# Queries and keys stored by heads in DRAM, weight transfers issued by SyncE in line with all other transfers

## The chip, the cores and the metric

One core of one Trainium2 chip. The metric is device time in microseconds of one execution of the whole step, median of three runs.

## What is computed

One inference step of a two-layer decoder, for a prompt of 1024 positions and for 8 sample tokens beside it. Each layer projects its input, runs attention on one half of the columns and a recurrent mix (RWKV-7) on the other, and then a feed-forward of width 4096. What the change touches is the path from the projection to attention:

```python
p = x @ w_comb                                   # x: (1024, 1024)
q = p[..., :512].reshape(B, T, 8, 64)
k = p[..., 512:1024].reshape(B, T, 8, 64)
v = p[..., 1024:1536].reshape(B, T, 8, 64)
q, k = rope(q, pos), rope(k, pos)                # halves of 32 of each head are rotated against each other
att = dilated_attention_prompt(q, k, v)          # windows (128,1), (512,4), (2048,16)
...
mix = jnp.concatenate([att, rw], -1) @ lp['w_out']
x1 = layer_norm(DEEPNORM_ALPHA * x + mix, ...)
h = jnp.square(jax.nn.relu(x1 @ lp['w_ff_up'])) @ lp['w_ff_down']
```

## The kernel before, in words

Each layer `l` is worked through in two halves `h` of 512 positions (the second with the 8 sample tokens). All large products are written by `dense_steps` (L365 to L372): the operands are split into a high and a low part of type fp32r, and each 128-row piece takes three matmuls (L370 high x high, L371 high weights x low input, L372 low weights x high input).

**Weights.** `Weights.fill` brings 820 pieces in the order of their use, nearly all 128x512 fp32 (256 KB). Of each, one transfer fills `wr` (L342, three buffers), ACT casts it to the high part `wh` (L343, four buffers), and DVE subtracts to give the low part `wl` (L344, four buffers). The transfer is issued by ACT itself, and `issue_after` puts it behind the cast of the second-last piece in ACT's order. All other transfers are issued by SP (SyncE).

**Order of the work.** TensorE's order is written out by hand: `Streams` merges six streams (dense products, attention, the two stages of the recurrence and others) by a model of their costs. The order on the other engines and on SP is made by the scheduler of the language. Each engine, and SP, works its list in order: what stands at the head and waits holds up what stands behind it.

**Queries and keys.** `in_proj` computes 128 columns of q and k for a pair of heads `p`, as a tile of 128 rows x 512 positions. Because of the rotation the rows lie as (half f, head d, index r), 2 x 2 x 32. L638 stores that tile as it is in `d_qkv[l][h][p, j]` (j = 0 for q, 1 for k), one transfer of 256 KB, 32 in all. `att_load` reads it back by heads: `heads(src)[hd]` picks two blocks of 32 rows of one head, and `stage` (L1497 to L1501) loads those 64 rows twice, once into each half of the 128 partitions of a tile `stg` (two buffers). ACT casts `stg` to the high parts `qS` (L1522) and `kS` (L1526), POOL subtracts to give the low parts (L1523, L1527). In the second half each pair of heads also loads `qf` and `kf` (L1514, L1515), each in two transfers, one a head, and the last 128 keys of the half before. In all there are 160 `stg` transfers (128 of 128 KB, 32 of 32 KB) and 32 of `qf` and `kf`.

```python
def heads(src):
    return src.rearrange("(f d r) t -> d f r t", f=2, d=2)
```

In the names of the rows, `wr`, `wh`, `wl` are a weight piece and its parts; `dps` is a dense product; `d_el`, `BL`, `XB`, `tm`, `X`, `XT` belong to the recurrence's triangular solve, which goes through DRAM several times; `kvc` is the cache of the sample tokens.

Of the kernel before, what the change touches and what calls it, by code (L numbers as in the profile page):

```python
# [28 lines left out]
HB = T // 2  # L29
# [115 lines left out]
class Streams:  # L145
# [24 lines left out]
    def note(self, *key):  # L170
        self.times[key] = self.now

    def after(self, *key, lat=0):
        return lambda: self.times[key] + lat if key in self.times else None
# [73 lines left out]
def body(ctx, tc, I, O):  # L248
    nc = tc.nc
    PE, V, A, G, S = nc.tensor, nc.vector, nc.scalar, nc.gpsimd, nc.sync  # L250
# [22 lines left out]
    def C(name):  # L273
        a, n = CAT[name]
        return cst[:, a:a + n]
# [24 lines left out]
    def both(f):  # L300
        return [[f(l, h) for h in range(2)] for l in range(DEPTH)]
# [5 lines left out]
    d_qkv = both(lambda l, h: dr.tile([4, 3, 128, HB], F32, name=f"d_qkv{l}{h}"))  # L307
# [7 lines left out]
    class Weights:  # L315

        def __init__(self, specs):  # L320
            self.pieces, self.first = [], []
            for srcs, m, dest in specs:
                self.first.append(len(self.pieces))
                self.pieces += [(src, m, dest) for src in srcs]
            self.first.append(len(self.pieces))
            self.out, self.copies = {}, []
            self.nl = self.i = self.kept = 0

        def fill(self, ahead=4):
            at = self.first[self.i]  # L330
            while self.nl < min(len(self.pieces), at + ahead):
                src, m, dest = self.pieces[self.nl]
                if dest is not None:
                    h, lo = dest()
                elif self.kept + sum(p[2] is None for p in self.pieces[at:self.nl]) == 4:
                    break
                else:
                    h = wp.tile([128, 4, 128], F32R, tag="wh", bufs=4, name="wh")
                    lo = wp.tile([128, 4, 128], F32R, tag="wl", bufs=4, name="wl")
                w = wp.tile([128, 4, 128], F32, tag="wr", bufs=3, name="wr")  # L340
                with tc.issue_after(self.copies[-2].ins) if len(self.copies) > 1 else nullcontext():
                    A.dma_start(w[:, :, :m], src)  # L342
                self.copies.append(A.copy(h[:, :, :m], w[:, :, :m]))  # L343
                V.tensor_tensor(lo[:, :, :m], w[:, :, :m], h.bitcast(F32)[:, :, :m], op=ALU.subtract)  # L344
                self.out[self.nl] = (h, lo)
                self.nl += 1
# [32 lines left out]
    def dense(items, kts, xhh, xll, evac):  # L379

        res = []
        yield (0, None, 0, "d")
        yield from dense_steps(items, kts, xhh, xll, res)
        for it, p in zip(items, res):
            r = evac(it, p)
            if r is not None:
                yield r
        for i, it in enumerate(items):
            yield (res[-1] if i == 0 else 0, ("d", 900 + 500 * i), 0, None)
# [8 lines left out]
    def proj_order():  # L398
        seq = [("z", 0)]
        for p in range(4):  # L400
            if p < 3:
                seq.append(("z", p + 1))
            seq.append(("a", p))
        return seq
# [147 lines left out]
    def in_proj(l, h, hook=None, tail=None, then=None):  # L552
# [27 lines left out]
        def z_ev(p, j):  # L580
            def put(c0, n, d):
                S.dma_start(d_z[l][h][p, j, :, c0:c0 + n], d[:, :n])
            return shifted(l, h, muv(4 * j + p), 128, 4 * j + p, put)
# [9 lines left out]
        for cs in ([[c] for c in first] if l > 0 else [ck]):  # L593
            end = cs[-1][0] + cs[-1][1] == HX[h]
            for i in ends[-2:] + ends[:-2] if held else ends:
                m, ev = lo[i]
                keep = not end and i in ends[-2:]
                w = held.pop(0) if held and not keep else W.take(keep)
# [15 lines left out]
        for kind, p in proj_order()[1:]:  # L614
            if kind == "a" and p == 3 and then is not None:
                yield from then()
            for j in range(3):
                w = W.take()
                if kind == "z":
                    ev = z_ev(p, j)  # L620
                    for c0, n in ck:
                        yield from dense([(w, 128, c0, n)], K8, xhc, xlc, ev)
                    continue
                seq = (2 * l + h) * 4 + p
                if j == 1 and seq > 0:
                    yield after("post", seq - 1)
                t = ap_.tile([128, HN[1]], F32, tag="qe", bufs=2, name="qe")

                def eva(it, pt):
                    _, _, c0, n = it  # L630
                    (V.tensor_copy if c0 else A.copy)(t[:, c0:c0 + n], pt[:, :n])
                for c0, n in CK[h]:
                    yield from dense([(w, 128, c0, n)], K8, xhc, xlc, eva)
                if j == 0 and h == 1:
                    t8 = ap_.tile([128, 5, 8], F32, tag="t8", name="t8")
                if j < 2:
                    rope(t, HN[h], tabs)
                    S.dma_start(d_qkv[l][h][p, j], t[:, 0:HB])  # L638
                    if j == 1:
                        S.dma_start(O["k_p"][l, p, :, h * HB:h * HB + HB], t[:, 0:HB])  # L640
                if h == 1 and j == 0:
                    if p == 0:
                        sq[l] = (rq.tile([128, 4, 32], F32, tag="q2", name="q2"), rq.tile([128, 4, 8], F32, tag="kn", name="kn"))
                        G.memset(sq[l][0], 0.0)
                    G.memset(t8[:, 1:4, :], 0.0)
                    for hd in range(2):
                        G.tensor_scalar(sq[l][0][:, p, hd:16:2], t[:, HB:HN[1]], C("hm")[:, hd:hd + 1], None, op0=ALU.mult)
                elif h == 1:
                    G.tensor_scalar(t8[:, (0, 4)[j - 1], :], t[:, HB:HN[1]], 1.0, None, op0=ALU.mult)
                    if j == 1:  # L650
                        G.tensor_scalar(sq[l][1][:, p, :], t[:, HB:HN[1]], 1.0, None, op0=ALU.mult)
            if kind == "a":
                qe[seq] = (l, h, p, t, t8 if h == 1 else None)
                note("qe", seq)
            note(kind, l, h, p)
# [832 lines left out]
    def att_load(l, h, p):  # L1488

        qS, qL, kS = [], [], []

        def heads(src):
            return src.rearrange("(f d r) t -> d f r t", f=2, d=2)

        def stage(src, hd, n):  # L1497
            t = ap_.tile([128, HB], F32, tag="stg", bufs=2, name="stg")[:, :n]
            for x in range(2):
                S.dma_start(t[64 * x:64 * x + 64], heads(src)[hd])  # L1500
            return t  # L1501

        def byres(t):
            return t.rearrange("p (j a c) -> p j c a", a=32, c=4)

        def inrow(t):
            return t.rearrange("p (j c a) -> p j c a", a=32, c=4)

        qf = kf = None
        if h == 1:  # L1510
            qf, kf = (ap_.tile([128, HB], F32, tag=x, name=x) for x in ("qf", "kf"))
            for hd in range(2):
                hs = slice(64 * hd, 64 * hd + 64)
                S.dma_start(qf[hs], heads(d_qkv[l][1][p, 0])[hd])  # L1514
                S.dma_start(kf[hs], heads(d_qkv[l][0][p, 1])[hd])  # L1515
        for hd in range(2):
            hs, ls = slice(64 * hd, 64 * hd + 64), slice(64 - 64 * hd, 128 - 64 * hd)
            q = ap_.tile([128, HB], F32R, tag=f"q{hd}", name="qS")
            ql = ap_.tile([128, HB], F32R, tag=f"ql{hd}", name="qL")
            k = ap_.tile([128, HB + 128], F32R, tag=f"k{hd}", name="kS")  # L1520
            t = stage(d_qkv[l][h][p, 0], hd, HB)
            A.copy(inrow(q), byres(t))  # L1522
            AQ.tensor_tensor(inrow(ql), byres(t), inrow(q.bitcast(F32)), op=ALU.subtract)  # L1523
            for src, c, n in [(d_qkv[l][0][p, 1][:, HB - 128:HB], 0, 128)] * h + [(d_qkv[l][h][p, 1], 128 * h, HB)]:
                t = stage(src, hd, n)
                A.copy(k[:, c:c + n], t)  # L1526
                AQ.tensor_tensor(k[ls, c:c + n], t[ls], k.bitcast(F32)[ls, c:c + n], op=ALU.subtract)  # L1527
            qS.append(q)
            qL.append(ql)
            kS.append(k)  # L1530
        return qS, kS, qL, qf, kf, R.now + 6000 + 1000 * (h + 1)
# [328 lines left out]
```

## Time and profile before

| | us |
|---|---|
| median of 3 runs (lowest, highest) | 3555.35 (3549.26, 3558.99) |
| the profiled execution | 3560.94 |
| its span, first to last instruction | 3559.1 |
| TensorE (PE) busy | 3202.7 (90%) |
| VectorE (DVE) busy | 2055.5 (58%) |
| ScalarE (ACT) busy, issues of transfers not counted | 1448.3 (41%) |
| GpSimd (POOL) busy | 979.3 (28%) |

[...] The profile has one page for the whole run, and views of the trace: who waited for whom, the chain of work that ended last, the instructions in order of time, and busy times of chosen stretches. Queue instructions carry a q (SPq, ACTq): they issue transfers and are not counted as busy. PE is busy in nine tenths of the span, so time is to be had from its idle tenth and from the stretches in which its clock is low.

### The profile page before, as it was taken

Reading aid. Unit: us, or ns where it says so; the run is one execution under the profiler, and the core shown is the slowest. Engines: PE = TensorE matmul, PEld = TensorE weight load, DVE = VectorE, ACT = ScalarE, POOL = GpSimd, SP = SyncE. Lnnn points to the kernel's source line nnn. Section 1 sums busy time; section 2 is a strip of 40 time slices with the busy share of each in tenths; the row PEclk is TensorE's granted clock in tenths of the full one; section 3 lists DMA queues with packets and bytes.
Section 4 is the critical chain, followed back from the end, with each engine's and each line's share of the span. In section 5 each row is a group of like instructions: output and inputs, shape, how many; then the busy total and the mean of one; then the engine's idle time right before and its main releaser. Section 6 shows DMA issues by size and latency. Waiting matters only on the chain. (4 is left out here: it accounts for less than half of the span.)

```text
span 3559.1 us, 65853 instructions
## 1 busy us (share of the span) xinstructions
PE 3202.7 (90%) x24732; PEld 2697.6 (76%) x24732; DVE 2055.5 (58%) x4703; ACT 1448.3 (41%) x3266; POOL 979.3 (28%) x1841
## 2 busy tenths in 40 slices
PE   8788897977999998888999999797797999889998
PEld 6567776765777687677899998685675677789998
DVE  4455554764554664567565457465764564685556
ACT  4345333443343344344443336343443333453334
POOL 2324233531111421435211113334412121340012
PEclk9899998988999999998999999898898999999999
DMA  7334343433443335442333235344243343333332
GB/s 219 107 113 124 115 115 103 129 95 99 117 112 85 106 97 163 139 150 68 86 98 92 80 98 154 117 126 133 71 118 100 111 113 91 117 101 91 94 90 84
DMA packets 366533, 393.55 MB, mean 111 GB/s; under 512 B 141848, under 2 KB 219112, under 8 KB 366216
## 3 DMA queue, kind: packets, MB, share of 16 engines
q10 hardware_dynamic: 121152, 213.44, 20.9%
q1 hardware_dynamic: 245064, 175.92, 16.9%
q8 instruction: 195, 3.19, 0.4%
q14 instruction: 122, 1.00, 0.1%
HBM read 325.30 MB, written 63.97 MB: 109 GB/s over the span
## 5 line engine op out<-in xcount | busy, mean ns | idle before, releaser
L370 PE MATMUL dps<-xh,wh 128*128 128x256 f32 (+3 forms) x2984 | 1006.9, 337 | 31.0 <-ACT xh L758 15.0
L371 PE MATMUL dps<-xl,wh 128*128 128x256 f32 (+3 forms) x2984 | 956.8, 321 | 10.4 <-DVE xl L759 8.6
L372 PE MATMUL dps<-xh,wl 128*128 128x256 f32 (+3 forms) x2984 | 953.3, 319 | 1.2 <-DVE wl L344 1.0
L344 DVE TENSOR_TENSOR wl<-wr,wh 128x512 fp32r<-128x512 f32 (+1 forms) x772 | 581.8, 755 | 501.3 <-ACT wh L343 485.6
L343 ACT CAST wh<-wr 128x512 fp32r<-128x512 f32 (+1 forms) x772 | 475.1, 616 | 844.4 <-PE dps L371 777.8
L370 PEld LDWEIGHTS dps<-xh,wh 128*128 128x128 f32 x2984 | 576.6, 193 | 106.4 <-issue 31.0
L371 PEld LDWEIGHTS dps<-xl,wh 128*128 128x128 f32 x2984 | 576.8, 193 | 46.3 <-DVE xl L759 12.5
L372 PEld LDWEIGHTS dps<-xh,wl 128*128 128x128 f32 x2984 | 575.6, 193 | 41.0 <-DVE wl L344 2.6
L370 PE MATMUL dps<-hh,wh 128*128 128x512 f32 (+2 forms) x1600 | 536.1, 335 | 5.4 <-DVE hh L941 3.6
L371 PE MATMUL dps<-hl,wh 128*128 128x512 f32 (+2 forms) x1600 | 513.1, 321 | 4.5 <-DVE hl L830 3.3
L372 PE MATMUL dps<-hh,wl 128*128 128x512 f32 (+2 forms) x1600 | 512.0, 320 | 0.0
L370 PEld LDWEIGHTS dps<-hh,wh 128*128 128x128 f32 x1600 | 303.5, 190 | 45.2 <-issue 17.7
L371 PEld LDWEIGHTS dps<-hl,wh 128*128 128x128 f32 x1600 | 304.1, 190 | 22.6 <-DVE hl L830 4.1
L372 PEld LDWEIGHTS dps<-hh,wl 128*128 128x128 f32 x1600 | 303.9, 190 | 22.6
L1209 POOL TENSOR_TENSOR tm<-BL,XB 32x15 f32<-32x15 f32 (+7 forms) x480 | 153.0, 319 | 496.5 <-DMA BL<-d_el 375.9
L973 DVE TENSOR_TENSOR t<-dps,t 128x256 f32<-128x256 f32 (+1 forms) x240 | 123.6, 515 | 161.1 <-PE dps L372 160.7
L1211 POOL TENSOR_TENSOR XB<-XB,tm 32x15 f32<-32x15 f32 (+7 forms) x480 | 154.6, 322 | 34.4
L726 POOL TENSOR_TENSOR ln<-ln,lsq 128x256 f32<-128x256 f32 (+1 forms) x112 | 91.2, 814 | 232.5 <-ACT lsq L724 229.9
L941 DVE CAST hh<-rl 128x256 fp32r<-128x256 f32 (+2 forms) x200 | 74.4, 372 | 108.6 <-ACT rl L940 105.4
L939 ACT ACTIVATE rl<-dps 128x256 f32<-128x256 f32 (+2 forms) x200 | 88.4, 442 | 102.2 <-PE dps L372 89.9
L715 POOL TENSOR_TENSOR t<-t,ln 128x256 f32<-128x256 f32 (+1 forms) x32 | 28.1, 913 | 352.1 <-ACT ln L709 352.1
L370 PE MATMUL dps<-hh,xh 128*128 128x256 f32 (+1 forms) x368 | 112.6, 306 | 13.3 <-DVE t L1006 7.2
(345 smaller groups left out, 5098.0 us busy)
## 6 DMA issues: line engine op xcount, KB each, us to landing
wr<-in_w_ff_up ACTq DMA_DIRECT2D x272, 256.0 KB
wr<-in_w_ff_down ACTq DMA_DIRECT2D x256, 256.0 KB
wr<-in_w_in ACTq DMA_DIRECT2D x220, 256.0 KB
stg<-d_qkv SPq DMA_DIRECT2D x128, 128.0 KB
wr<-in_w_out ACTq DMA_DIRECT2D x64, 256.0 KB
z<-d_z SPq DMA_DIRECT2D x24, 384.0 KB
d_qkv<-qe SPq DMA_DIRECT2D x32, 256.0 KB
kvc<-in_cache_k SPq DMA_DIRECT2D x32, 256.0 KB
```

Of the source, the lines that this page charges most:

```text
L343: self.copies.append(A.copy(h[:, :, :m], w[:, :, :m]))
L344: V.tensor_tensor(lo[:, :, :m], w[:, :, :m], h.bitcast(F32)[:, :, :m], op=ALU.subtract)
L370: PE.matmul(p[:m, :n], wh[:, wk % 4, :m], hi, start=(i == 0), stop=False)
L371: PE.matmul(p[:m, :n], wh[:, wk % 4, :m], lo, start=False, stop=False)
L372: PE.matmul(p[:m, :n], wl[:, wk % 4, :m], hi, start=False, stop=(i == last))
L715: G.tensor_tensor(t, t, self.cm[:, c0:c0 + n], op=ALU.subtract)
L726: G.tensor_tensor(s2, s2, sq, op=ALU.add)
L939: A.activation(r, p[:, :n], AF.Relu)
L941: V.tensor_copy(hh[:, c0:c0 + n], r)
L973: V.tensor_tensor(to, p[:, :n], to, op=ALU.add)
L1209: G.tensor_tensor(tv, bc(BL[:, 17 * j + 1:17 * j + 2], [(1, m), (0, j + 1)]), bc(XB[:, 16 * j:16 * j + 1], [(0, m), (1, j + 1)]), op=ALU.mult)
L1211: G.tensor_tensor(xv, xv, tv, op=ALU.add)
```

## The change

The tile of queries or keys is stored in four transfers of 32 rows, so that in DRAM the 64 rows of a head lie together (head d, half f, index r). The reads by head become plain blocks of 64 rows, and `qf` and `kf` become one transfer of 128 rows each. The weight transfers are issued by SP, without the condition on the cast of the second-last piece.

```diff
-            self.out, self.copies = {}, []
+            self.out = {}
...
-                with tc.issue_after(self.copies[-2].ins) if len(self.copies) > 1 else nullcontext():
-                    A.dma_start(w[:, :, :m], src)
-                self.copies.append(A.copy(h[:, :, :m], w[:, :, :m]))
+                S.dma_start(w[:, :, :m], src)
+                A.copy(h[:, :, :m], w[:, :, :m])
                 V.tensor_tensor(lo[:, :, :m], w[:, :, :m], h.bitcast(F32)[:, :, :m], op=ALU.subtract)
...
                     rope(t, HN[h], tabs)
-                    S.dma_start(d_qkv[l][h][p, j], t[:, 0:HB])
+                    for f in range(2):
+                        for d in range(2):
+                            a, b = 64 * f + 32 * d, 64 * d + 32 * f
+                            S.dma_start(d_qkv[l][h][p, j, b:b + 32], t[a:a + 32, 0:HB])
...
-        def heads(src):
-            return src.rearrange("(f d r) t -> d f r t", f=2, d=2)
-
         def stage(src, hd, n):
             t = ap_.tile([128, HB], F32, tag="stg", bufs=2, name="stg")[:, :n]
             for x in range(2):
-                S.dma_start(t[64 * x:64 * x + 64], heads(src)[hd])
+                S.dma_start(t[64 * x:64 * x + 64], src[64 * hd:64 * hd + 64])
...
-            for hd in range(2):
-                hs = slice(64 * hd, 64 * hd + 64)
-                S.dma_start(qf[hs], heads(d_qkv[l][1][p, 0])[hd])
-                S.dma_start(kf[hs], heads(d_qkv[l][0][p, 1])[hd])
+            S.dma_start(qf, d_qkv[l][1][p, 0])
+            S.dma_start(kf, d_qkv[l][0][p, 1])
```

TensorE's order is the same in both kernels. SP's list grows from 1277 to 2177 transfers: 820 weight transfers come to it, the stores of queries and keys go from 32 to 128, `qf` and `kf` from 32 to 16. The three places below show what moves.

SP in the first layer's second half, where the second pair of heads is loaded for attention, before (of the loads of `qf` and `kf` the second pair is shown):

```order
L1514 DMA qf<-d_qkv_109 64x1x512
L1515 DMA kf<-d_qkv_108 64x1x512
L1500 DMA stg<-d_qkv_109 64x1x512 x4
L1399 DMA d_rw_93<-y 128x256
L1500 DMA stg<-d_qkv_108 64x1x128 x2
L1092 DMA lo_8869<-d_lo_105 128x2x264
L1500 DMA stg<-d_qkv_109 64x1x512 x4
```

and now:

```order
L1509 DMA qf<-d_qkv_109 128x512
L1510 DMA kf<-d_qkv_108 128x512
L1497 DMA stg<-d_qkv_109 64x512 x4
L1497 DMA stg<-d_qkv_108 64x128
L1399 DMA d_rw_93<-y 128x256
L1497 DMA stg<-d_qkv_108 64x128
L339 DMA wr<-in_w_ff_up 128x512
L1497 DMA stg<-d_qkv_109 64x512 x2
L339 DMA wr<-in_w_ff_up 128x512
L1092 DMA lo_8911<-d_lo_105 128x2x264
```

The loads keep their places, their shape is now 64x512 in one block, and two weight transfers stand among them, the first behind the store `d_rw<-y`.

SP in the first layer's first half, where a tile of queries is stored, before:

```order
L1215 DMA d_el_115<-XB 32x16x16
L638 DMA d_qkv_108<-qe 128x512
L1220 DMA X<-d_el_115 64x4x64
L1216 DMA d_el_116<-tm 32x16x16
L1220 DMA X<-d_el_115 64x4x64
L1399 DMA d_rw_92<-y 128x256
L1221 DMA XT<-d_el_116 64x4x64 x2
L1500 DMA stg<-d_qkv_108 64x1x512 x2
```

and now:

```order
L1215 DMA d_el_115<-XB 32x16x16
L638 DMA d_qkv_108<-qe 32x512
L1220 DMA X<-d_el_115 64x4x64 x2
L1216 DMA d_el_116<-tm 32x16x16
L638 DMA d_qkv_108<-qe 32x512 x2
L1221 DMA XT<-d_el_116 64x4x64 x2
L638 DMA d_qkv_108<-qe 32x512
L1399 DMA d_rw_92<-y 128x256
L339 DMA wr<-in_w_in 128x512
L1497 DMA stg<-d_qkv_108 64x512 x2
```

The four parts of the store are spread among the transfers of the recurrence, and the last part, `d_rw<-y` and a weight transfer stand ahead of the load.

ACT at the first of these places, before:

```order
L343 CAST wh<-wr 128x512
L1526 CAST kS<-stg 128x512
L342 DMA wr<-in_w_ff_up 128x512
L721 ACTIVATE ln_7566<-t 128x256
L1522 CAST qS<-stg 128x512
L1302 COPY T_7905<-pT_7896 128x256
```

and now:

```order
L1521 CAST kS<-stg 128x512
L724 ACTIVATE lsq<-t 128x256
L1569 ACTIVATE E,mx<-E,mx 128x640
L340 CAST wh<-wr 128x512
L1517 CAST qS<-stg 128x512
L721 ACTIVATE ln_7610<-t 128x256
L1302 COPY T_7947<-pT_7938 128x256
```

The weight transfer that stood behind the cast of the keys is gone from ACT, and the cast of the keys stands three places earlier; the copy `T` that TensorE needs still stands behind the cast of the queries.

## Rows read from the trace of the kernel before

**Rows 1.** The page: busy times, and the chain that ended last by line.

```profile
PE 3202.7 (90%) x24732; PEld 2697.6 (76%) x24732; DVE 2055.5 (58%) x4703; ACT 1448.3 (41%) x3266; POOL 979.3 (28%) x1841
...
PE dps L370 7%; PE dps L371 7%; PE dps L372 7%; DMA stg<-d_qkv 3%; DVE t L756 1%; DMA wr<-in_w_out 0%; PE pS L1554 0%; DVE t L737 0%; DVE wl L344 0%; PE pX L1280 0%; POOL tm L1209 0%; DVE ln L725 0%; PE po L1611 0%; SPq L1500 0%; POOL XB L1211 0%
```

**Rows 2.** The chain that ended last, from 2200 to 2720 us: start, us, what.

```profile
by line: DMA stg<-d_qkv 19.6%; PE dps L370 12.1%; PE dps L372 10.2%; PE dps L371 10.2%; issue 2.8%; PE pS L1554 2.2%; SPq L1500 2.0%; DVE t L737 1.6%; PE pX L1280 1.5%; PE po L1611 1.2%; POOL kS L1527 1.2%; POOL qL L1523 1.2%; PE pS L1565 1
...
2236.54 3.04 DMA d_qkv<-qe
2241.29 12.67 DMA stg<-d_qkv
...
2698.09 7.96 DMA stg<-d_qkv
```

**Rows 3.** Who waited for whom, ACT: total us, times, longest.

```profile
ACT kS L1526 <- DMA stg<-d_qkv: 191.7, 33, 16.6
ACT qS L1522 <- DMA stg<-d_qkv: 120.7, 19, 15.3
```

**Rows 4.** Instructions of ACT, 703 to 731 us: start, us, name, count, idle before.

```profile
709.33 0.60 ACT L343 CAST wh<-wr 128x512 fp32r<-128x512 f32 x1
721.17 0.62 ACT L1526 CAST kS<-stg 128x512 fp32r<-128x512 f32 x1 [11.23 <-DMA stg<-d_qkv]
721.19 0.34 ACTq L342 DMA_DIRECT2D wr<-in_w_ff_up  x1
...
727.53 1.09 ACT L1522 CAST qS<-stg 128x512 fp32r<-128x512 f32 x1 [5.42 <-DMA stg<-d_qkv]
...
728.52 0.37 ACT L1302 COPY T<-pT 128x256 f32<-128x256 f32 x1
```

**Rows 5.** The same stretch on SP's queue.

```profile
704.59 10.31 SPq L1500 DMA_DIRECT2D stg<-d_qkv  x4
```

**Rows 6.** The same stretch on PE.

```profile
728.94 1.12 PE L1280 MATMUL pX<-XT,T 64*64 64x64 f32 x16 [15.38 <-ACT T L1302]
```

**Rows 7.** Busy time in 16 stretches: us, PE, PEld, DVE, ACT, POOL (counts), PEclk, DMA, GB/s.

```profile
263.90:269.40 5.50, 0.00 (x0) 0.00 (x0) 0.00 (x0) 1.29 (x5) 3.24 (x3) 0.96 0.11 37
...
866.10:888.60 22.50, 0.02 (x1) 0.00 (x0) 0.73 (x2) 1.36 (x3) 1.26 (x1) 0.58 0.27 83
...
sum 151.30, PE 0.15 PEld 0.06 DVE 10.05 ACT 28.90 POOL 25.14; mean PE 0.01 PEld 0.00 DVE 0.63 ACT 1.81 POOL 1.57
```

**Rows 8.** The same view of the 16 stretches right behind those.

```profile
328.30:334.30 6.00, 5.08 (x33) 3.69 (x33) 0.84 (x4) 2.90 (x7) 2.37 (x3) 0.50 0.26 68
...
2266.40:2272.40 6.00, 6.00 (x40) 5.96 (x41) 1.52 (x2) 0.46 (x1) 1.74 (x5) 0.77 0.55 170
...
sum 90.40, PE 88.47 PEld 73.37 DVE 41.37 ACT 27.68 POOL 41.12; mean PE 5.53 PEld 4.59 DVE 2.59 ACT 1.73 POOL 2.57
```

**Rows 9.** The chain that ended last: two transfers of the nearest shapes.

```profile
2803.03 2.65 DMA kvc<-in_cache_v
...
2893.37 3.29 DMA ST<-in_state_wkv
```

**Rows 10.** Single lines: count, min/median/max ns of one issue, first and last start.

```profile
L638 SPq DMA_DIRECT2D d_qkv<-qe x32: 319/332/2788, 73.4 to 2430.7; - x32
L1425 SPq DMA_DIRECT2D iup<-in_vres_up x8: 342/576/592, 1123.0 to 2653.3; - x8
L342 ACTq DMA_DIRECT2D wr<-in_w_ff_up x272: 334/334/372, 684.3 to 3500.0; - x136
```

**Rows 11.** Instructions in order of time from 0 us, SP's queue.

```profile
0.72 5.77 SPq L507 DMA_DIRECT2D t<-in_x  x8
```

**Rows 12.** Who waited for whom, POOL: total us, times, longest.

```profile
POOL tm L1209 <- DMA BL<-d_el: 375.9, 24, 50.1
```

**Rows 13.** Who waited for whom, SP's queue: total us, times, longest.

```profile
SPq L1198 <- DVE LB L1191: 179.9, 16, 30.2
SPq L1215 <- POOL XB L1211: 152.4, 28, 17.2
SPq L1399 <- DVE y L1398: 125.1, 25, 12.9
```

## The prediction, made before the changed kernel ran

> **What bounds the kernel now.** I read the page first. PE is busy for 3202.7 us of the 3559.1 us span [rows 1], so the kernel is bound by PE, and what can be won is its 356.4 us of idle time, and the time it works at a low clock. In the chain that ended last one transfer stands out among lines of matmuls: `stg<-d_qkv`, the read of queries and keys, with 3% of the span [rows 1]. The second view is that chain between 2200 and 2720 us, the second layer's attention loads: there `stg<-d_qkv` is the largest item of all, 19.6% of 520 us, 102 us, in ten pieces of which the first lasts 12.67 us and the last 7.96 us, each from issue to landing [rows 2]. So one piece takes 10.2 us in the mean, for 128 KB.
>
> The third view is who waits for that transfer: ACT, 52 times, 191.7 + 120.7 = 312 us [rows 3]. ACT is not the bound, so I looked at one place to see whether this reaches PE. At 709.9 us ACT is done with a weight's cast, and its next instruction, the cast of the keys, waits 11.23 us for `stg`; soon after, the cast of the queries waits another 5.42 us; only then comes the copy `T` [rows 4]. PE needs that `T` and stands idle for 15.38 us [rows 6]. Nothing is wrong with `T` itself: it stood behind two casts whose data had not landed. SP shows the other side: its four issues of `stg` began at 704.59 us and took 10.31 us [rows 5], so SP too was held up.
>
> I followed every idle time of PE back in this way. In 16 of them the larger part is `stg` in flight: in 15 ACT (or POOL behind it) waits for it, and in the one at 866 us a `kvc` transfer that PE needs was held behind four `stg` issues on SP. They sum to 151 us in which PE did 0.15 us of work [rows 7]. [...] Ceiling of what faster reads can return: 151 + 34 = 185 us.
>
> **The change part by part.**
>
> *Reads by head.* The 160 `stg` transfers keep their number, places and bytes; the DRAM side becomes one block of 64 rows. No row shows this very shape. The nearest is `ST<-in_state_wkv`, 128 KB into 64 partitions, 3.29 us; another load lands in 2.65 us [rows 9]. Upper bound: nothing changes, 10.2 us. I take 3.29 us, since it has the same bytes and partitions. Then 1 - 3.29/10.2 = 68% of each wait goes; with 2.65 us it would be 74%, with 10.2 us none. Worked at the one place: the first pair of loads is issued from 704.6 us, would land by about 704.6 + 0.5 + 3.3 = 708.4 us, and ACT comes for it at 709.9 us, so the 11.23 us wait would be gone altogether. Sum: 0.68 x 185 = **126 us less**, between 0 and 185. The rate of 128 KB in 10.2 us, 13 GB/s, against 40 GB/s for `ST`, is why I put the cause in the shape. [...]
>
> *Stores in four.* One store issue took 0.332 us; a transfer of 32 partitions takes 0.576 us [rows 10], so the fourth part is issued 4 x 0.58 - 0.33 = 2.0 us later than the one store was. Over 32 stores that is 64 us of SP at most; at least 0, where other work covers it. A store is in the chain with 3.04 us at only the first of the ten pieces [rows 2], so I charge 2.0 us at about a quarter of the 16 stalls: **8 us more**. That the four lie in series is rival D.
>
> *`qf` and `kf`.* 16 issues fewer and two fewer reads at a time beside `stg`; it is within the first item.
>
> *Weights from ACT to SP.* 820 issues of 0.334 us [rows 10], 274 us in all, leave ACT and come to SP. On ACT this was never long on the path (no line of ACT's queue is in the chain's list [rows 1]); I count 0; at most, two of them stand inside a stall, as the one at 721.19 us and its like [rows 4], so 16 x 2 x 0.334 = 11 us less. On SP each weight ahead of a transfer delays it by 0.33 us. The transfers that matter are the solve's, some five steps in each of 32 units: 160 x 0.33 = 53 us if all were on the path. POOL waits for that solve 375.9 us [rows 12] and yet no such line reaches 1% of the chain [rows 1], so it is mostly covered; I take a quarter, **13 us more**, with bounds 0 and 53. SP also has a new wait: a weight at its head waits for its `wr` buffer, which DVE frees with L344 three pieces back, and behind it stand the solve's and attention's transfers, for which POOL and ACT wait. One such wait is up to the 3.9 us in which PE uses a piece (3202.7/820); the list puts a weight where its buffer is expected free, so I add nothing, and its bad case belongs to B.
>
> *Order on ACT, DVE, POOL.* It moves by a few places; no price, and its cover is the same slack.
>
> Sum: -126 + 8 + 13 = **-105 us**. Against the profiled execution's 3560.9 us that is 3456 us; the median of the runs is 5.6 us lower, 3555.35, so I predict **3450 us**.
>
> **The rivals.**
>
> *A, half is taken back.* With `stg` early, PE comes to the next wait sooner, above all to what follows the solve's round trips (POOL's 375.9 us, longest 50.1 [rows 12]), which no part of this change shortens. For it: PE's other 356 - 151 = 205 us of idle time have such causes. Against it: these chains start from PE and ACT work that also comes earlier. If half of the 126 us comes back as new idle time: 3555 - 63 + 21 = 3513 us.
>
> *B, SP becomes the bound (slower).* SP's list is in order. Before, it stood 179.9 + 152.4 + 125.1 = 457 us in 69 waits for the recurrence's results, up to 30.2 us at a time [rows 13], and no weight was behind them. Now a weight is, as behind `d_rw<-y` in the order. At 3.9 us a weight, three `wr` and three further `wh` buffers hold six, 23 us ahead when full, 12 us when only `wh` is. A wait longer than that starves PE. It decides for slower when 105 + 11 = 116 us of those 457 us, a quarter, come through. Against it: the mean wait is 6.6 us, and they were long since SP had nothing else to do. With half of them, 228 us: 3450 + 228 = 3678 us; with a third, 152 us: 3602 us.
>
> *C, the reads are not slow by their shape*, but by waiting for DRAM or for other transfers. Then they stay at 10 us, only the small costs remain, 21 us, with ACT's 11 us against them: 3555 + 10 = 3565 us, within the resolution. Against it: the 13 GB/s and SP's own held-up issues [rows 5].
>
> *D, the four parts of a store run one after another (slower).* A store takes 3.04 us from issue to landing [rows 2]; three more in series ahead of the loads of 16 stalls are 3 x 3.04 x 16 = 146 us instead of my 8: 3450 + 138 = 3588 us. Against it: eight loads of 256 KB were issued back to back in 5.77 us [rows 11], so transfers of one queue overlap. [...]
>
> **How the numbers follow.** Forecast 0.70, A 0.15, B 0.08, C 0.05, D 0.02. Forecast and A are faster: 0.85. A measurement of this kernel can tell 0.3%, 11 us, from no change. C lies within it: 0.05; B and D are slower: 0.10. The range: 3400 us is where nearly all of the ceiling less the small costs comes back (185 - 21 = 164 us would be 3391 us); the upper end 3540 us takes in A and a weaker form of it; B, C, D and the far end below, 2 in 10, are left out.
>
> **What would show it.** Right: ACT's waits for `stg` fall from 312 to about 100 us; `stg` leaves the chain's list; the idle times at 713, 2400, 2533 and 2684 us are gone, and idle PE falls from 356 to about 270 us; the mean granted clock rises over 0.949. ACT's queue issues no weight, SP's issues 820. B shows as PE or ACT's cast waiting for `wr`, with SP at a wait for `LB`, `XB` or `y`; A as PE waits for DVE, POOL or `d_el` that were not there; C as `stg` pieces still of 8 to 15 us; D as a long gap from a store to the load behind it. The prediction is wrong if `stg` lands in 3 us and the time does not fall by at least 15 us.

## The result, and the profile after

The changed kernel takes **3294.51 us** (median of 4 runs, 3289.59 to 3296.90) against 3555.17 us for the kernel before (median of 4): ratio 0.9266, 95% interval 0.9249 to 0.9284. That is 261 us less. The prediction said faster, by 105 us; the time lies 105 us below the lower end of its range.

The page of the changed kernel, busy times and the chain that ended last by line:

```profile
PE 3148.2 (96%) x24732; PEld 2660.9 (81%) x24732; DVE 2051.3 (62%) x4703; ACT 1448.4 (44%) x3266; POOL 983.0 (30%) x1841
...
PE dps L367 9%; PE dps L368 8%; PE dps L369 8%; DVE t L756 1%; PE pS L1549 1%; DMA wr<-in_w_out 0%; DVE wl L341 0%; DMA ST<-in_state_wkv 0%; DVE ln L725 0%; PE pX L1280 0%; PE pO L1356 0%; PE po L1606 0%; PE pS L1560 0%; PE pET L1583 0%; DV
```

`stg<-d_qkv` was the first line of this chain that is no matmul, with 3% [rows 1]; now it is not listed. PE is idle for 3294.7 - 3148.2 = 146.5 us where it was 356.4 us, and it is busy for 54.5 us less with the same 24732 matmuls [rows 1]. The two are 209.9 + 54.5 = 264.4 us, the whole difference of the spans (3559.1 - 3294.7). The busy time fell because of the clock: PE was busy for 207 us at a granted clock of 0.50 before and is for 107 us now, and half of the difference, 50 us, is nearly all of the 54.5 us. The cores' view, span and mean granted clock, of the kernel before and then of the changed one:

```profile
core 0: 3559.1 us, clock 0.949
```

```profile
core 0: 3294.7 us, clock 0.980
```

Who waited for whom in the changed kernel (total us, times, longest):

```profile
ACT kS L1521 <- DMA stg<-d_qkv: 34.1, 22, 3.5
ACT qS L1517 <- DMA stg<-d_qkv: 20.0, 15, 3.5
ACT sq L1120 <- DMA z<-d_z: 15.4, 11, 2.8
PE pds L1739 <- DMA kvc<-in_cache_k: 1.2, 1, 1.2
```

The waits for `stg` were 191.7 and 120.7 us, up to 16.6 us each [rows 3]; they are 54 us, at most 3.5 us each. The last two rows are about transfers that the change does not touch. In the kernel before they read:

```profile
ACT sq L1120 <- DMA z<-d_z: 36.7, 13, 12.3
PE pds L1744 <- DMA kvc<-in_cache_k: 22.5, 1, 22.5
```

So transfers with nothing of their own changed also come sooner. The row on `kvc` is the better sign: in the run with the layout alone (below), which gives the whole gain, it is 6.6 us, and the row on `z` still 29.7 us. The place that the prediction worked at, 728.94 us before [rows 4 to 6], is at 617.88 us now. ACT, in order of time (start, us, name, idle before):

```profile
611.09 0.62 ACT L1521 CAST kS<-stg 128x512 fp32r<-128x512 f32 x1 [2.09 <-DMA stg<-d_qkv]
...
613.92 1.15 ACT L1517 CAST qS<-stg 128x512 fp32r<-128x512 f32 x1 [0.53 <-DMA stg<-d_qkv]
...
615.26 0.38 ACT L1302 COPY T<-pT 128x256 f32<-128x256 f32 x1
```

and PE:

```profile
617.67 0.28 PE L369 MATMUL dps<-hh,xl 128*128 128x256 f32 x1
617.88 0.68 PE L1280 MATMUL pX<-XT,T 64*64 64x64 f32 x16
```

The casts wait 2.09 and 0.53 us where they waited 11.23 and 5.42 us, the copy `T` is done 2.2 us before PE comes for it, and PE does not stop where it stood for 15.38 us. PE's instructions are the same in the same order, so each of the 16 stalls can be looked up. The windows view of the changed kernel, from 5 us before to 1 us behind the instruction that ended each stall (two pairs overlap; columns as in rows 7):

```profile
612.90:618.90 6.00, 5.56 (x58) 4.34 (x57) 5.96 (x11) 5.42 (x14) 4.67 (x5) 1.00 0.31 99
...
2071.60:2077.60 6.00, 2.15 (x10) 1.11 (x9) 3.12 (x6) 3.62 (x8) 5.44 (x11) 0.87 0.79 250
...
sum 96.00, PE 85.99 PEld 71.11 DVE 58.62 ACT 54.15 POOL 48.56; mean PE 5.37 PEld 4.44 DVE 3.66 ACT 3.38 POOL 3.03
```

PE is idle for 10.0 of these 96 us, 3.85 us of it in the one window at 2071 us; right ahead of the 16 instructions themselves it is idle for 7 us, where it was about 151 us [rows 7].

### The profile page after: what moved, and what is told of

The parts are those of the page before. It is cut to its first block, busy times and chain, and to the rows that moved or that the text cites. A ratio compares the mean times of both kernels' runs of the same rounds, so it can differ in the third digit from the quotient of the medians.

```text
span 3294.7 us, 66426 instructions
## 1 busy us (share of the span) xinstructions
PE 3148.2 (96%) x24732; PEld 2660.9 (81%) x24732; DVE 2051.3 (62%) x4703; ACT 1448.4 (44%) x3266; POOL 983.0 (30%) x1841
## 5 line engine op out<-in xcount | busy, mean ns | idle before, releaser
L367 PE MATMUL dps<-xh,wh 128*128 128x256 f32 (+3 forms) x2984 | 995.3, 334 | 16.4 <-ACT wh L340 9.6
L341 DVE TENSOR_TENSOR wl<-wr,wh 128x512 fp32r<-128x512 f32 (+1 forms) x772 | 571.4, 741 | 361.3 <-ACT wh L340 337.3
L367 PEld LDWEIGHTS dps<-xh,wh 128*128 128x128 f32 x2984 | 569.0, 191 | 88.0 <-issue 26.5
L368 PEld LDWEIGHTS dps<-xl,wh 128*128 128x128 f32 x2984 | 569.7, 191 | 44.8 <-DVE xl L759 12.8
L369 PEld LDWEIGHTS dps<-xh,wl 128*128 128x128 f32 x2984 | 568.8, 191 | 40.5 <-DVE wl L341 3.3
```

The source lines that it names most:

```text
L367: PE.matmul(p[:m, :n], wh[:, wk % 4, :m], hi, start=(i == 0), stop=False)
L368: PE.matmul(p[:m, :n], wh[:, wk % 4, :m], lo, start=False, stop=False)
L369: PE.matmul(p[:m, :n], wl[:, wk % 4, :m], hi, start=False, stop=(i == last))
```

## The experiments

All times are medians on one chip per group; each ratio is to the kernel before on that chip. The theory that stood after the comparison of the two profiles: **Q**, a read in two blocks occupies two DMA engines for long, and delays not only who waits for it but whatever else passes through them. The two are an estimate from the trace of the kernel before: from 320.69 to 323.79 us and from 1624.16 to 1627.36 us four `stg` reads and nothing else are in flight, and the mean busy share of the 16 DMA engines is 0.13, so 0.13 x 16 = 2.1 engines. Rivals: the weights (W), the place of the rows in DRAM rather than the shape of the reads, and that ACT's wait for `stg` is the whole effect.

| kernel | us | ratio to before (95%) |
|---|---|---|
| changed kernel | 3294.51 | 0.9266 (0.9249 to 0.9284) |
| the same, with the last group | 3301.83 | 0.9235 (0.9222 to 0.9247) |
| layout alone | 3297.03 | 0.9249 (0.9230 to 0.9267) |
| weights on SP alone | 3570.64 | 1.0019 (1.0009 to 1.0029) |
| old layout, reads in blocks of 32 rows | 3302.50 | 0.9262 (0.9248 to 0.9275) |
| changed, weights on ACT in line | 3288.51 | 0.9219 (0.9203 to 0.9235) |
| changed, eight stores | 3314.52 | 0.9292 (0.9278 to 0.9306) |
| eight stores, reads of four blocks | 3415.65 | 0.9574 (0.9558 to 0.9590) |
| changed, idle copies of two blocks | 3489.18 | 0.9779 (0.9764 to 0.9793) |
| changed, idle copies of one block | 3328.29 | 0.9334 (0.9316 to 0.9353) |
| weights on SP, slow reads on ACT | 3604.48 | 1.0079 (1.0066 to 1.0093) |
| old layout, rows apart | 3303.54 | 0.9237 (0.9224 to 0.9251) |
| the same, weights on ACT in line | 3296.92 | 0.9219 (0.9207 to 0.9232) |

**1. The layout alone.** The kernel before with the diff's second, third and fourth parts, without the first:

```diff
...
                 with tc.issue_after(self.copies[-2].ins) if len(self.copies) > 1 else nullcontext():
                     A.dma_start(w[:, :, :m], src)
...
-                    S.dma_start(d_qkv[l][h][p, j], t[:, 0:HB])
...
+                            S.dma_start(d_qkv[l][h][p, j, b:b + 32], t[a:a + 32, 0:HB])
...
-                S.dma_start(t[64 * x:64 * x + 64], heads(src)[hd])
+                S.dma_start(t[64 * x:64 * x + 64], src[64 * hd:64 * hd + 64])
```

> The kernel before with the new layout alone (stores in four, plain reads by head, qf and kf whole); weights stay on ACT, behind the cast of the second-last piece. Theory L (layout): the slow reads cost more than the 16 stalls in which stg itself was the wait, since they also held up the other transfers; the layout then gives nearly all of the 261 us, 3295 us +- 25. If the weights on SP cost the 13 us that the prediction charged, it is 3282 us. Rival W (weights): a good share, 60 us or more, came from taking the weights off ACT, where they stood behind ACT's waits for stg; then 3355 us or more. By the prediction's own first term with nothing beyond it, 3437 us.

Measured: 3297 us, ratio 0.9249, whose interval overlaps that of the changed kernel. The layout gives all of the gain; W falls.

**2. The weights alone.** The kernel before with the first part only:

```diff
-                with tc.issue_after(self.copies[-2].ins) if len(self.copies) > 1 else nullcontext():
-                    A.dma_start(w[:, :, :m], src)
-                self.copies.append(A.copy(h[:, :, :m], w[:, :, :m]))
+                S.dma_start(w[:, :, :m], src)
+                A.copy(h[:, :, :m], w[:, :, :m])
```

> The kernel before with the weights on SP alone; queries and keys are stored and read as before. Theory L: no gain to speak of, 3555 us +- 20. Rival W: 3495 us or less. Third case: the weights now stand behind the issues of stg on SP, which took up to 3.6 us each before, so PE runs out of weights: slower, 3600 us or more; the layout would then be what makes the second part of the change harmless.

Measured: ratio 1.0019, 7 us slower by the ratio and 4.6 us by the medians, in the expected band. The third case did not come, although the issues of `stg` on SP were still held up. Single lines of this kernel (count, ns min/median/max of one issue) and ACT's waits:

```profile
L1499 SPq DMA_DIRECT2D stg<-d_qkv x160: 482/510/4509, 78.8 to 2704.9; - x160
```

```profile
ACT kS L1525 <- DMA stg<-d_qkv: 202.5, 34, 16.4
ACT qS L1521 <- DMA stg<-d_qkv: 128.5, 20, 14.9
```

**3. Shape or place.** The changed kernel with the old layout, and reads of 32 rows in one block:

```diff
...
-                            S.dma_start(d_qkv[l][h][p, j, b:b + 32], t[a:a + 32, 0:HB])
+                    S.dma_start(d_qkv[l][h][p, j], t[:, 0:HB])
...
-                S.dma_start(t[64 * x:64 * x + 64], src[64 * hd:64 * hd + 64])
+                for f in range(2):
+                    S.dma_start(t[64 * x + 32 * f:64 * x + 32 * f + 32], src[64 * f + 32 * hd:64 * f + 32 * hd + 32])
...
```

> The changed kernel with the old layout in DRAM: one store of 128 rows for each tile, and each read by head in two transfers of one block of 32 rows (stg 320 transfers for 160, qf and kf 64 for 16, stores 32 for 128). If the two blocks within one transfer made the reads slow, the time is that of the changed kernel, 3295 us, and up to 25 us more for the 112 issues more: 3295 to 3320 us, and stg lands in 2 to 3 us. If it is the place of the rows in DRAM, stg still lands in about 8 us and the time is 3450 us or more. If the store in four parts cost something (8 us in the prediction), it is 3287 us.

Measured: 3302 us, ratio 0.9262. The rows lie in DRAM as before the change, and the gain is there: it is the two blocks within one transfer that made the reads slow. The 208 reads more and 96 stores fewer change nothing that can be told.

**4. Weights on ACT, in line.**

```diff
-                S.dma_start(w[:, :, :m], src)
+                A.dma_start(w[:, :, :m], src)
```

> The changed kernel with the weights issued by ACT, in line with its own work, without the condition on the cast of the second-last piece. Theory L: 3295 us +- 15, ACT has 56% of the span idle and takes 820 x 0.334 = 274 us of issues without harm. If ACT's issues cost on the path: 3310 to 3340 us. If weights on SP cost something (13 us in the prediction), 3282 us.

Measured: ratio 0.9219, which is 17 us less than the changed kernel's 0.9266 and 6 us less than its 0.9235 in the last group. These two differ by 0.0031 themselves, so kernels of different groups can't be told apart more finely; the last group takes the question up again.

**5. Eight stores, and 6. four blocks.** First each tile in eight stores of 16 rows, then the same with the rows so placed that a read is one transfer of four blocks:

```diff
-                            a, b = 64 * f + 32 * d, 64 * d + 32 * f
-                            S.dma_start(d_qkv[l][h][p, j, b:b + 32], t[a:a + 32, 0:HB])
+                            for s in range(2):
+                                a, b = 64 * f + 32 * d + 16 * s, 64 * d + 32 * f + 16 * s
+                                S.dma_start(d_qkv[l][h][p, j, b:b + 16], t[a:a + 16, 0:HB])
```

```diff
-                                a, b = 64 * f + 32 * d + 16 * s, 64 * d + 32 * f + 16 * s
+                                a, b = 64 * f + 32 * d + 16 * s, 64 * f + 32 * s + 16 * d
...
+            return src.rearrange("(g d r) t -> d g r t", g=4, d=2)
...
-                S.dma_start(t[64 * x:64 * x + 64], src[64 * hd:64 * hd + 64])
+                S.dma_start(t[64 * x:64 * x + 64], heads(src)[hd])
...
```

> The changed kernel with each tile of queries and keys stored in eight transfers of 16 rows for four of 32; the layout and the reads stay. It prices the splitting and is the kernel to hold the next one against. 128 issues more on SP, 73 us at the 0.576 us that the prediction took. If what it charged holds (8 us for 96 more), 10 us more than the changed kernel: 3305 us. If splitting costs nothing on the path, as the run with one store and reads in blocks of 32 rows suggests: 3295 us +- 8. If the parts run one after another (rival D of the prediction): 3400 us or more.

> As the run with eight stores, but with the rows in DRAM so that a read by head is one transfer of four blocks of 16 rows (before: two blocks of 32), for stg, qf and kf. If the number of blocks sets the number of DMA engines that work on a transfer, stg comes in with four engines, lands in 4 to 5 us (half of the 7.9 us median of before) and the time lies between: 3330 to 3430 us. If any split into blocks is as slow as two, 3500 us or more. If only the pair of two was bad, as for the run with eight stores.

Measured: 3315 us with eight stores, above both cases that were expected without rival D (3305 us, and 3295 +- 8). In ratio that is 0.0026 or 0.0057 above the changed kernel's two measurements, 9 to 20 us for 128 stores more; the 3400 us of rival D are far off. With four blocks 3416 us, 101 us above its control: 40% of the 253 us that separate the control from the kernel before. ACT's waits for `stg` lie between too:

```profile
ACT kS L1527 <- DMA stg<-d_qkv: 82.6, 28, 8.9
ACT qS L1523 <- DMA stg<-d_qkv: 60.8, 18, 7.0
```

How long `stg` itself was in flight can be counted in the trace, from the end of an issue to the transfer's last semaphore increment, over its 128 transfers of 128 KB; beside it the 64 transfers `d_el<-LB` of the solve, whose shape no kernel changed:

```text
                                  stg: increments  median  90th percentile   d_el<-LB: 90th percentile
before                                          3    7.91            11.88                        6.50
four blocks                                     5    4.97             7.37                        2.32
changed kernel                                 16    2.21             3.06                        2.36
idle copies of two blocks                      16    2.36             6.27                        5.03
idle copies of one block                       16    2.26             2.97                        2.55
slow reads on ACT's queue                       3    8.52            12.25                        5.76
old layout, rows apart                         16    2.23             2.94                        2.51
```

The increments go with the shape: 3 for two blocks, 5 for four, 16 for plain reads. How many engines worked on a single transfer, they do not show.

With four blocks `d_el<-LB` lands as in the changed kernel, but not every other transfer does: the 90th percentile of the 32 `kvc<-in_cache_k` is 8.07 us there and 3.41 us in the control.

**7. and 8. Idle copies.** The changed kernel with two more transfers behind each pair of `stg` reads, of the same bytes, to DRAM that nobody reads:

```diff
...
                 S.dma_start(t[64 * x:64 * x + 64], src[64 * hd:64 * hd + 64])
+            for x in range(2):
+                u = d_idle[idle[0] % 16]
+                idle[0] += 1
+                S.dma_start(u[:, :n], src.rearrange("(f d r) t -> d f r t", f=2, d=2)[hd])
```

and in the control `src[64 * hd:64 * hd + 64]` in the last line.

> The changed kernel with, behind each pair of stg reads, two further transfers of the same bytes that nobody reads: they copy the same part of d_qkv, taken as two blocks of 32 rows as before, to scratch in DRAM. Theory Q (queue): transfers of two blocks fill few engines for long and hold up those behind them and SP's own issues, whoever waits for them; then a good part of the loss comes back though nobody waits for these copies: 60 us or more above the run with plain copies, and other transfers (wr, d_el, kvc) land late as before the change. Rival: only ACT's wait for stg itself counted, and the rest of the gain was what followed from it; then within 20 us of the run with plain copies.

> The same with the idle copies taken as one block of 64 rows: the control, which prices the added bytes (20 MB read and written) and the 160 issues more. SP has slack, so 3295 to 3320 us by either theory.

Measured: 3489 us with two blocks, 3328 us with one, which is over the 3320 us that was expected of the control. The shape of transfers whose data nobody reads costs 161 us. The trace has 3 increments for each of the copies of two blocks, with a median of 6.50 us in flight, and 16 with 2.18 us for those of one. The page and ACT's waits with two blocks:

```profile
PE 3205.9 (92%) x24732; PEld 2704.1 (78%) x24732; DVE 2049.4 (59%) x4703; ACT 1447.9 (42%) x3266; POOL 973.4 (28%) x1841
```

```profile
ACT wh L341 <- DMA wr<-in_w_in: 80.1, 28, 20.0
ACT kS L1526 <- DMA stg<-d_qkv: 76.8, 24, 14.2
ACT sq L1121 <- DMA z<-d_z: 32.7, 12, 7.0
```

and with one:

```profile
PE 3166.5 (95%) x24732; PEld 2675.5 (80%) x24732; DVE 2053.3 (62%) x4703; ACT 1450.0 (43%) x3266; POOL 984.4 (30%) x1841
```

```profile
ACT wh L341 <- DMA wr<-in_w_in: 49.1, 29, 6.6
ACT kS L1526 <- DMA stg<-d_qkv: 32.9, 20, 4.2
ACT sq L1121 <- DMA z<-d_z: 17.0, 13, 3.3
```

ACT waits longer for the weights, `z` and the plain reads of `stg` behind the idle copies, up to 20.0 us for one weight; `kvc`, which the expectation named too, is not late (PE waits 1.1 us for the keys). ACT's wait for its own slow read as the whole effect falls. Theory Q holds for the time in flight, which is counted from the end of an issue: the 90th percentile of the plain `stg` is 6.27 us against 2.97 us in the control, that of `d_el<-LB` 5.03 against 2.55 us (the table above). But there is a second way, which Q does not name: SP waits for the landing of the copies, although nobody reads them. SP's queue with two blocks and in the control:

```profile
SPq L1502 <- DMA d_idle<-d_qkv: 35.6, 21, 6.7
SPq L1199 <- DMA d_idle<-d_qkv: 10.5, 6, 2.8
```

```profile
SPq L1502 <- DMA d_idle<-d_qkv: 2.7, 4, 1.2
```

L1502 issues the copies themselves, L1199 the store `d_el<-LB`. Over all lines of SP it is 107 us with two blocks and 2.7 us with one. All transfers of a kernel, whoever issues them, count their landing on the same eight semaphores (in the kernel before 1277 of SP and 820 of ACT, 262 or 263 on each); going by the increments in the traces (3 for each of the 160 `stg` reads before, 16 for each in the changed kernel), a semaphore's next transfer is issued only when the one before it has landed, and SP, whose list is in order, stands there meanwhile. Of the 107 us, 84 are such waits; in the other 23 a copy waits for another copy. How the 161 us divide between transfers that are late in flight and an SP that stands was not separated.

The idle time of PE is 281.6 us against 169.3 us in the control (spans 3487.5 and 3335.8 us), and its busy time 39.4 us more: the loss has the two parts that the change's gain has.

**9. Another queue.** The run with the weights on SP, with the slow reads issued by ACT:

```diff
-                S.dma_start(t[64 * x:64 * x + 64], heads(src)[hd])
+                A.dma_start(t[64 * x:64 * x + 64], heads(src)[hd])
...
-                S.dma_start(qf[hs], heads(d_qkv[l][1][p, 0])[hd])
+                A.dma_start(qf[hs], heads(d_qkv[l][1][p, 0])[hd])
```

and `kf` in the same way.

> The run with the weights alone on SP, with the reads of queries and keys (two blocks of 32 rows, as before) issued by ACT, so on another queue than all other transfers. Theory Q (transfers of two blocks hold up what stands behind them in their own queue): the solve's, the weights' and kvc's transfers land as in the changed kernel, and stg itself waits for its own kind alone, so that 100 us or more of the 261 us come: 3470 us or less. Rival: the two engines are what is clogged, whichever queue it is, or ACT now stands in the issues as SP did: 3540 us or more.

Measured: 3604 us, ratio 1.0079; the rival, whose two halves (clogged engines, ACT standing in the issues) this run does not separate. The solve's transfers on SP's queue are late although no slow read is in it (the table above, 5.76 us), ACT waits for `stg` as long as before, and a single issue on ACT now takes up to 5.3 us:

```profile
ACT kS L1525 <- DMA stg<-d_qkv: 190.1, 35, 17.8
ACT qS L1521 <- DMA stg<-d_qkv: 131.5, 20, 13.2
PE pds L1743 <- DMA kvc<-in_cache_k: 14.0, 1, 14.0
```

```profile
L1499 ACTq DMA_DIRECT2D stg<-d_qkv x160: 488/490/5292, 78.4 to 2736.7; - x160
```

The solve's transfers are late in flight (5.76 us against 2.36 us in the changed kernel), so something behind the two queues is shared, and my wording of Q ("in their own queue") falls. That it is the two engines is not shown. The semaphores are shared in any case: over all lines of SP's queue, SP stands 149 us in 50 waits for the landing of reads that ACT issued, each time before a transfer that uses the same semaphore; in the kernel before it stood 68.5 us for its own. The issue of the weights, which have no data in common with these reads:

```profile
SPq L341 <- DMA stg<-d_qkv: 37.4, 11, 10.9
```

So the run moved the slow reads to another queue without freeing SP of them, and what another queue alone would give is not shown.

**10. and 11. Rows apart.** The old layout and the single store, the two blocks of a head read row by row in turn, so that the outermost dimension is 32 long; then with the weights on ACT. The order of rows within a head changes for queries and keys alike, and their products stay.

```diff
...
-                            S.dma_start(d_qkv[l][h][p, j, b:b + 32], t[a:a + 32, 0:HB])
+                    S.dma_start(d_qkv[l][h][p, j], t[:, 0:HB])
...
+            return src.rearrange("(f d r) t -> d r f t", f=2, d=2)
...
-                S.dma_start(t[64 * x:64 * x + 64], src[64 * hd:64 * hd + 64])
+                S.dma_start(t[64 * x:64 * x + 64], heads(src)[hd])
```

> The changed kernel with the old layout and the single store, but a head's rows read in the order r, f (row by row from the two blocks in turn) as one transfer; the order of rows within a head is then another one for queries and keys alike. The rows lie in DRAM as they did before the change. If only the outermost number of blocks matters (32 here for 2), stg lands in 2 to 3 us, and with 96 stores fewer the time is that of the changed kernel or up to 15 us less: 3285 to 3300 us. If reads that hop between the blocks are slow, 3400 us or more.

> The same with the weights issued by ACT in line. From the run with ACT's issues and the changed layout (ratio 0.9219 against 0.9266) 15 us less than the kernel with rows apart and weights on SP: 3265 to 3290 us, the fastest kernel of this study. If ACT's gain came from relief of SP alone, of which the fewer stores already give some: within 5 us of that kernel.

**12. The changed kernel in the same group.**

> The changed kernel once more, as a base for the two kernels of this group that go beyond it: ratio to before 0.9266 +- 0.002, 3290 to 3305 us.

Measured: 3303.5, 3296.9 and 3301.8 us; ratios 0.9237, 0.9219, 0.9235. The changed kernel's own ratio lies outside the 0.9266 +- 0.002 that was expected, and the 15 us less with the weights on ACT (3265 to 3290 us) did not come. One changed order of dimensions in the read does all that the new layout does, with no store split. The 96 stores fewer return nothing measurable, and weights on ACT 6 us that the intervals (0.9207 to 0.9232 against 0.9224 to 0.9251) do not separate. No version beats the changed kernel by more than can be told.

## Why the prediction was right in direction and wrong in size

The mechanism was the right one: two blocks of a head made the reads slow (a median of 7.91 us in flight against 2.21 us), PE stood behind ACT's waits for them, and the gain is theirs alone. The sum was mis-sized in four terms. From the two profiles, matching PE's instructions one by one:

| term | predicted us | measured us |
|---|---|---|
| idle in the 16 stalls | 0.68 x 151 = -103 | 151 to 7: -144 |
| the rest of PE's idle time | 0 | 205 to 139: -66 |
| low clock (PE busy) | 0.68 x 34 = -23 | -54.5 |
| stores and SP | +21 | in the terms above, not visible |
| sum | -105 | -264 |

- **The ceiling of 185 us, under "What bounds the kernel now", is the step that failed.** It counted a stall only where `stg` itself was the wait that ended last. The other 205 us were set aside as having other causes (rival A says so). The idle copies show that transfers of this shape cost time without ACT or PE waiting for them: 161 us, through other transfers that are late in flight and through SP, which stands until they have landed. I had the sign of it in hand, SP's four issues in 10.31 us [rows 5], and took it for SP's affair alone. How the 261 us divide between the reads' own lateness and that of the others was not separated: the idle copies make `stg` late as well.
- **The 68%, under "Reads by head".** I shortened each wait in proportion to the landing, yet found at the one worked place that its wait would be gone altogether, since a read landing before ACT asks for it costs nothing. That holds for nearly all 16: 95% went. The 3.29 us itself was fair: the trace counts a median of 2.21 and a 90th percentile of 3.06 us.
- **The low clock.** I took 34 us, right behind the 16 stalls: in those 90.4 us PE was busy for 88.5 us at a granted clock between 0.50 and 0.77 [rows 8], 0.615 in the mean weighted by length, and 0.385 x 88.5 = 34. In the whole kernel before it cost half of 207 us, 104 us, and it costs 54 us now. With some of the other idle time gone as well, PE's busy time fell by 54.5 us and the granted clock rose to 0.980.
- **Stores in four, +8 us, and weights on SP, +13 us.** Neither is seen in the sum. 128 stores more cost 9 to 20 us, 96 fewer return nothing; the weights cost 7 us with the slow reads in place, and without them 6 us or nothing, which the intervals do not tell.

The rivals: A (half taken back) did not come. The idle time that grew at any PE instruction sums to 55 us, none of it over 5 us, and is within the net 66 us. B (SP as the bound) did not come either; SP now waits with a weight at its head for its buffer, and its waits for the recurrence fell instead of growing [rows 13]. Two of the lines of SP's queue, changed kernel:

```profile
SPq L339 <- DVE wl L341: 997.6, 414, 23.4
...
SPq L1198 <- DVE LB L1191: 40.8, 18, 5.9
```

Those 998 us are time in which the weights are already ahead. C falls with the run with reads of 32 rows, D with the eight stores. Of the signs that the prediction named, the waits for `stg` (54 us for "about 100"), the chain, the clock and the four vanished stalls came; idle PE of "about 270 us" was 146.5.

## What to carry to other kernels

Before pricing a transfer's shape, look at the outermost dimension of its access pattern: swapping two dimensions of the read was here worth as much as a new layout in memory (ratio 0.9237 against 0.9235). A transfer that stays long in flight can be paid for by other transfers too (161 us here, for copies that nobody reads), and by the queue that stands until it has landed, so its price is not the sum of the compute engines' waits that name it; look also for late transfers that nobody changed and for issues that take long, and leave the ceiling open upward. And a wait ends at the moment the data is wanted: compare landing with need, place by place, rather than shortening every wait by one factor.

## What had not been expected of the hardware

A transfer in two blocks, which shows 3 increments, delays those that show 16: with idle copies of two blocks the 90th percentile of `d_el<-LB` was 5.03 us, with plain ones 2.55 us, and its shape is the same in both. Why they are late in flight, no run shows. Issuing the slow reads from ACT gave no relief (1.0079 against 1.0019); SP stood 149 us for their landing all the same, on semaphores that the two queues share, and a single issue held ACT for up to 5.3 us, where the median is 0.49 us. A read lands sooner step by step with the number of its blocks: the median in flight was 7.91, 4.97 and 2.21 us for two blocks, four, and a plain read.
